# Where the second tile's norm stands at a change of sublayer

## The chip, the cores and the metric

The program runs on one core of a Trainium2 chip. TensorE (PE) multiplies and transposes, VectorE (DVE) and ScalarE (ACT) work elementwise, GpSimd (POOL) computes small powers here, SyncE (SP) starts most of the transfers. Each engine takes its instructions in the order in which they stand in its queue, and waits for others by semaphores. The metric is the time of one execution on the device in microseconds (us), as the median of several runs.

## What is computed

Two residual networks one after the other over 256 tokens of 1024 features, in float32: a modulated block of depth 2, and a block of four layers with another mixer each. Cut to the skeleton:

```python
def first_block(x, c, ...):
    for l in range(2):
        mod = (silu(c) @ w_ada[l] + b_ada[l]).reshape(B, 9, D)
        h = modulate(rms_norm(x, norm_gain[l, 0]), mod[:, 0], mod[:, 1])
        x = x + 0.5 * mod[:, 2] * swiglu(h, ...)           # ffn00, ffn10
        h = modulate(rms_norm(x, norm_gain[l, 1]), mod[:, 3], mod[:, 4])
        x = x + mod[:, 5] * hybrid_mixer(h, ...)           # mixer 0, mixer 1
        h = modulate(rms_norm(x, norm_gain[l, 2]), mod[:, 6], mod[:, 7])
        x = x + 0.5 * mod[:, 8] * swiglu(h, ...)           # ffn01, ffn11

def second_block(h, positions, ...):
    for i in range(4):    # short convolution, recurrence, latent attention, short convolution
        h = h + mixer_i(rms_norm(h, mix_norm[i]))
        h = h + swiglu_ffn(rms_norm(h, ffn_norm[i]), ...)
```

`modulate(h, shift, scale)` is `h * (1 + scale) + shift`. The hybrid mixer holds two attentions of eight heads, a pooling branch, and a gated sum of the three. There are fourteen sublayers, and so thirteen changes from one to the next. At the first five (into mixer 0, ffn01, ffn10, mixer 1, ffn11) the norm has a modulation; at the other eight it has a gain alone.

## The kernel before

The 256 tokens are two tiles of 128, tile 0 and tile 1. `tokens(t)` is a generator over the steps of a tile through all fourteen sublayers; `drive` picks which tile takes its next step. A step yields the weight it held TensorE for: 8 for an up product or a projection, 4 for a down product, or it yields a wait. `drive` keeps how far tile 0 is ahead (`done[0] - done[1]`): from `lag` on tile 1 is picked first. A wait `("wait", a, b)` lets tile 0 go on while it is at most `a` ahead, and tile 1 once tile 0 is at least `b` ahead. What `drive` and the generators emit is the program's order; the framework then places the instructions into each engine's queue, by when it thinks that they can run, and in that it may let instructions of different steps pass each other.

A weight granule (`granule`, L223 to L237) is loaded by SP's queue (512 KB) and split into two float32r parts whose sum it is: ScalarE rounds (`hl`, L234), VectorE takes the rest (L235). `product` (L246 to L254) makes three float32r matmuls of each float32 product; one up product of 512 columns is 24 matmuls into a bank `mm`. Down products add into two banks `dn`. Tile 0 splits a weight chunk, and tile 1 uses it after it.

A change of sublayer: after the last down product `residual` (L309) multiplies the result by the gate (L316, where there is one) and adds it to x (`kept`, L317). `row_stats` (L320) squares x on ScalarE (L326), takes the power -0.5 on GpSimd (L330), and, where the norm has a modulation, leaves the normalised rows (VectorE, L334, `xn`). Then `norm_mod` (L337) or `norm_gain` (L353) begins with the wait `CHAIN`: eight transposes on TensorE (`transposes`, L268, into two `tr` banks), eight scalings on ScalarE (L348) and a split (L279 on ScalarE, L281 on VectorE), or for the gain eight multiplications on each (L291, L294). It ends with the wait `READY`. The next product takes those parts.

`CHAIN = ("wait", 7, 10)`: tile 1's norm may be emitted when tile 0 is 10 ahead, that is after tile 0's norm and the first and second product (8 + 8) of the next sublayer. `lag` is set by `lead`, to 8 (`MID`) or 14 (`END`).

Beside this the first block needs the modulation: `ada_cols` (L368) and `ada_row` (L389) load 512 KB each into one of three `araw` buffers and reduce them on VectorE (L376 for shift and scale, L400 for the gate). `fill` hands such tasks out during tile 0's steps, in a list for the sublayers ahead.

In the attention, `attend` (L509) takes a head norm (`head_norm`: reduction L497, power L304 on GpSimd, multiplication L501), transposes the probabilities into `tr` banks, copies them out (L551 on VectorE) and transposes again through matmuls (L560).

Of the kernel before, what the change touches and what calls it, by code (L numbers as in the profile page):

```python
# [15 lines left out]
PSUM = bass.MemoryType.PSUM  # L16
# [12 lines left out]
# ---------------------------------------------------------------- host layout  # L29


def pack(w, kt, cols):
    """Columns `cols` of w [K, N] as granules [K / (128 kt), 128, kt, len(cols)]."""
    w = w[:, cols]
    k, n = w.shape
    return np.ascontiguousarray(w.reshape(k // (P * kt), kt, P, n).transpose(0, 2, 1, 3))


def consts():
    """Matrices that depend on shapes alone, side by side: [128, n]."""  # L40
# [11 lines left out]
def bands():  # L52
    """What a window of tokens adds to each mean less the token itself: [128, 12, 128]."""
# [14 lines left out]
def arrange(a):  # L68
    """The inputs as the program reads them: the same numbers, laid out."""
# [94 lines left out]
# -------------------------------------------------------------------- program  # L164


class Program:
    """Two tiles of 128 tokens, each a generator over its steps. The second follows the first, so that what one
    tile waits for is hidden by products of the other. A step yields the products it held the tensor engine for
    (in tiles of split weights), or a wait: how far tile 0 may be ahead to go on, how far it must be for tile 1."""  # L170
# [20 lines left out]
    # --- tiles  # L191
# [29 lines left out]
    # --- weights: a granule [128, kt, n] from DRAM, as pairs of float32r parts that add up to it  # L221
# [17 lines left out]
    def weight(self, t, key, srcs):  # L239
        """The rows of k-tiles of a weight chunk: split by the first token tile, used by both."""  # L240
# [5 lines left out]
    def product(self, out, xs, ws, start=True, stop=True):  # L246
        """out += sum over k of xs[k].T @ ws[k] in float32: out is [(ap, column slice)]."""
# [16 lines left out]
    def transposes(self, src, n, tag="tr"):  # L264
        """src [128, n * 128] -> PSUM [128, n, 128], block by block."""
# [9 lines left out]
    def split(self, src, n, scale=1.0, tag="s4"):  # L275
        """float32 [128, n, 128] times scale, as float32r parts (lists over n)."""
# [9 lines left out]
    def split_cols(self, src, n, gain):  # L286
        """float32 [128, n, 128] times a gain per partition and block."""
# [11 lines left out]
    def rsqrt(self, ss, scale, n=1):  # L299
        """(ss * scale + EPS) ** -0.5"""  # L300
# [6 lines left out]
    # --- between sublayers: residual, 1 / rms of the rows of x, norm  # L307

    def residual(self, t, acc, mod, normed):  # L309
        """x += acc (times the gate); then 1 / rms, and x / rms where the norm wants that."""  # L310
# [7 lines left out]
        self.row_stats(t, acc, normed)  # L318

# [17 lines left out]
    def norm_mod(self, t, A, B):  # L337
        """Parts of (x / rms * A + B).T by k-tile."""
# [14 lines left out]
    def norm_gain(self, t, gain):  # L353
        """(x * gain).T and 1 / rms, which the products' results are scaled by."""
# [8 lines left out]
    CHAIN = ("wait", 7, 10)  # L363
    READY = ("wait", 0, 16)

    # --- modulation: c_act @ w_ada + b_ada; shift and scale by feature, the gate as a row on every partition

    def ada_cols(self, state, l, s, i, k):  # L368
        """Two blocks of 128 features of the shift or scale."""
# [19 lines left out]
    def ada_row(self, state, l, s, k):  # L389
        """Two k-tiles of the gate, partial sums by partition."""  # L390
# [20 lines left out]
    def ada_tasks(self, l, s, rows):  # L411
        """Steps that leave rows of shift, scale, gate of sublayer s of layer l in self.mods: (heavy, step)."""
# [19 lines left out]
    # --- feed-forward  # L432
# [52 lines left out]
    # --- attention  # L485

    def head_norm(self, ps, heads, factor=None):
        """PSUM [128, heads * dh], times a factor per token (given with its square), over the rms of each head."""
# [15 lines left out]
    def head_cols(self, y, gain, o):  # L504
        """[128 tokens, 512] -> [128 features, 4, 128 tokens] times a gain per feature."""
        self.nc.scalar.activation(o, self.transposes(y, 4), AF.Copy, scale=gain)
        return o

    def attend(self, t, logits, vs, bias_group, done, dv=64, scale=1.0):  # L509
        """Eight heads, four at a time, in steps. bias_group(g): per head what TensorTensor adds to the logits (or,  # L510
# [729 lines left out]
```

## Time and profile before

| | |
|---|---|
| median of 3 runs | 2535.97 us (2534.54 to 2538.55) |
| profiled execution | span 2533.8 us; it is not one of the three, and has no time beside its span |
| TensorE busy | 2430.1 us, 96% |
| VectorE, ScalarE, GpSimd busy | 64%, 50%, 3% |
| TensorE's granted clock | 0.9 or more of full speed in all but two of 40 slices |
| mean traffic | 197 GB/s, 499 MB |

In the profile a row of a timeline is one instruction or a run of the same: its start in us from the beginning of the span, its length, the engine, the line of the kernel, the operation, which tile it writes and which it reads, the shape, the count; in brackets the time for which the engine stood idle ahead of it, and what ended that. L254 are the matmuls of `product`, L268 the transposes. The clock is given as a share of full speed.

### The profile page before, as it was taken

The page shows a single profiled execution, that of the slowest core. Times are in us where ns is not written, and L with a number is a line of the kernel's source. Part 1 is how long each engine was busy: PE and PEld are TensorE (multiplying, and loading weights), DVE is VectorE, ACT ScalarE, POOL GpSimd, SP SyncE. Part 2 cuts the span into 40 slices and gives each one's busy share as a digit, 9 for nine tenths or more (in the row PEclk, how much of TensorE's full clock was granted, in tenths as well). Part 3 has the DMA queues.
Part 4 walks back from the last instruction along what each step waited for, and adds up shares of the span by engine and source line. Part 5 has one row for each costly group of instructions (what it writes and reads, how often), then busy time and mean ns, then how long its engine had stood idle before and what let it go on. Part 6 is the DMA issues. An engine that isn't in the chain of part 4 may idle for free.

```text
span 2533.8 us, 31294 instructions
## 1 busy us (share of the span) xinstructions
PE 2430.1 (96%) x11394; PEld 1989.6 (79%) x11394; DVE 1625.8 (64%) x2504; ACT 1272.7 (50%) x2007; POOL 86.3 (3%) x114
## 2 busy tenths in 40 slices
PE   6999999999999999999999999988998899999999
PEld 4877878878877878887888888776887688888887
DVE  7868687667568557666457654697545755467553
ACT  4535544554454465446445544675545554465443
POOL 0000100000000021000000000000000100000000
PEclk8999999999999999999999999998999999999999
DMA  8888675569568555445555465543553446555551
GB/s 316 327 295 301 228 260 167 177 229 329 181 214 322 187 183 175 134 161 181 190 176 200 155 202 189 172 160 108 200 179 117 133 135 198 166 193 190 202 184 63
DMA packets 137789, 499.02 MB, mean 197 GB/s; under 512 B 15842, under 2 KB 15842, under 8 KB 137635
## 3 DMA queue, kind: packets, MB, share of 16 engines
q1 hardware_dynamic: 135650, 490.86, 56.6%
q0 software_dynamic: 1984, 6.16, 0.8%
q8 instruction: 89, 1.46, 0.2%
q14 instruction: 66, 0.53, 0.1%
HBM read 495.92 MB, written 1.05 MB: 196 GB/s over the span
## 4 chain that ended last, share of the span: by engine, by line
PE 81%; DVE 6%; DMA 2%; ACT 2%; issue 2%; POOL 1%; SPq 0%; DVEq 0%; POOLq 0%; ACTq 0%
PE mm L254 53%; PE dn L254 21%; PE tr L268 3%; DVE hl L235 2%; PE tr L560 1%; POOL tiny L304 1%; DMA araw<-in_w_shift 1%; DMA araw<-in_w_mod 1%; PE tr L912 0%; ACT hl L234 0%; PE tr L254 0%; PE dn L589 0%; DVE s L922 0%; PE tr L408 0%; PE tr L678 0%
## 5 line engine op out<-in xcount | busy, mean ns | idle before, releaser
L254 PE MATMUL mm<-hl,s 128*128 128x512 f32 (+1 forms) x6774 | 1620.3, 395 | 45.2 <-ACT s L279 19.4
L254 PEld LDWEIGHTS mm<-hl,s 128*128 128x128 f32 x6774 | 1268.9, 190 | 319.3 <-ACT s L279 23.8
L235 DVE TENSOR_TENSOR hl<-raw,hl 128x1024 fp32r<-128x1024 f32 (+1 forms) x792 | 950.3, 1216 | 134.5 <-ACT hl L234 33.5
L234 ACT ACTIVATE hl<-raw 128x1024 fp32r<-128x1024 f32 (+1 forms) x792 | 830.2, 1056 | 365.9 <-PE mm L254 166.0
L254 PE MATMUL dn<-hl,s 128*128 128x512 f32 x2712 | 667.6, 397 | 8.9 <-ACT s L279 8.1
L254 PEld LDWEIGHTS dn<-hl,s 128*128 128x128 f32 x2712 | 497.1, 188 | 113.3 <-ACT s L279 10.2
L449 DVE SCALAR_TENSOR_TENSOR s<-mm,tiny,s 128x256 f32<-128x256 f32 x88 | 42.3, 480 | 266.5 <-ACT s L445 266.5
L445 ACT ACTIVATE s<-mm,tiny 128x256 f32<-128x256 f32 x88 | 41.8, 475 | 259.8 <-PE mm L254 259.7
L268 PE MATMUL tr<-kept,s 128*128 128x128 f32 x860 | 145.9, 279 | 14.7 <-DVE s L334 6.4
L268 PEld LDWEIGHTS tr<-kept,s 128*128 128x128 f32 x860 | 112.9, 144 | 54.7 <-DVE s L334 6.2
L445 ACT ACTIVATE s<-mm 128x256 f32<-128x256 f32 x88 | 33.6, 382 | 213.9 <-PE mm L254 213.9
L376 DVE CUSTOM_DVE_ANT_0 araw<-araw,s 128x1024 f32<-128x1024 f32 x88 | 107.0, 1218 | 38.9 <-DMA araw<-in_w_shift 23.4
L447 DVE TENSOR_TENSOR s<-mm,s 128x256 f32<-128x256 f32 x88 | 36.9, 420 | 133.8 <-ACT s L445 133.8
L281 DVE TENSOR_TENSOR s<-tr,s 128x256 fp32r<-128x256 f32 (+1 forms) x188 | 81.1, 432 | 43.4 <-ACT s L279 43.2
L279 ACT ACTIVATE s<-tr 128x256 fp32r<-128x256 f32 (+1 forms) x196 | 78.5, 401 | 40.7 <-PE tr L268 40.7
L330 POOL TENSOR_TENSOR tiny<-tiny,kept 128x1 f32<-128x1 f32 x30 | 19.7, 658 | 1960.4 <-DVE tiny L328 1930.8
L400 DVE SCALAR_TENSOR_TENSOR acc<-araw,kept,acc 128x1024 f32<-128x1024 f32 x48 | 61.5, 1280 | 11.7 <-DMA araw<-in_w_mod 11.2
L538 ACT ACTIVATE s<-s,tiny 128x128 f32<-128x128 f32 (+1 forms) x80 | 35.4, 444 | 51.2 <-DVE tiny L535 48.2
L326 ACT ACTIVATE dn<-kept 128x512 f32<-128x512 f32 x60 | 35.9, 598 | 49.6 <-DVE kept L317 49.6
L294 DVE SCALAR_TENSOR_TENSOR s<-tr,kept,s 128x128 fp32r<-128x128 f32 x154 | 42.9, 343 | 16.6 <-ACT s L291 16.6
L777 ACT ACTIVATE s<-mm 128x512 f32<-128x512 f32 x24 | 14.3, 597 | 73.7 <-PE mm L254 73.7
L317 DVE TENSOR_TENSOR kept<-kept,dn 128x512 f32<-128x512 f32 x56 | 36.9, 681 | 22.1 <-PE dn L254 21.9
(177 smaller groups left out, 999.6 us busy)
## 6 DMA issues: line engine op xcount, KB each, us to landing
raw<-in_gu SPq DMA_DIRECT2D x352, 512.0 KB, 5.4
raw<-in_dn SPq DMA_DIRECT2D x176, 512.0 KB, 5.9
raw<-in_win SPq DMA_DIRECT2D x104, 512.0 KB, 5.3
araw<-in_w_scale SPq DMA_DIRECT2D x48, 512.0 KB, 7.5
araw<-in_w_mod SPq DMA_DIRECT2D x48, 512.0 KB, 6.9
raw<-in_cin SPq DMA_DIRECT2D x48, 512.0 KB, 5.2
araw<-in_w_shift SPq DMA_DIRECT2D x40, 512.0 KB, 7.6
raw<-in_wbr SPq DMA_DIRECT2D x24, 512.0 KB, 5.5
```

Source lines behind the costliest of these rows:

```text
L234: nc.scalar.activation(hi, raw, AF.Copy)
L235: nc.vector.tensor_sub(lo, raw, hi.bitcast(F32))
L254: nc.tensor.matmul(ap, lhsT=x, rhs=w[:, sl], start=start and k == 0 and i == 0, stop=stop and k == last and i == 2)
L268: self.nc.tensor.transpose(bank[:, j, :], src[:, j * P : (j + 1) * P], self.ident)
L279: nc.scalar.activation(hi, src, AF.Copy, scale=scale)
L281: nc.vector.tensor_sub(lo, src, hi.bitcast(F32))
L294: nc.vector.scalar_tensor_tensor(lo[:, j, :], src[:, j, :], g, hi[:, j, :].bitcast(F32), op0=ALU.mult, op1=ALU.subtract)
L317: nc.vector.tensor_add(x[:, sl], x[:, sl], acc[j])
L376: nc.vector.tensor_tensor_reduce(out=raw, in0=raw, in1=self.crow, scale=1.0, scalar=0.0, op0=ALU.mult, op1=ALU.add, accum_out=state["sum"] ...
L400: nc.vector.scalar_tensor_tensor(acc, raw, self.cact[:, q : q + 1], acc, op0=ALU.mult, op1=ALU.add)
L445: nc.scalar.activation(h, ps[:, :256], AF.Silu, scale=1.0 if r is None else r)
L449: nc.vector.scalar_tensor_tensor(h, ps[:, 256:], r, h, op0=ALU.mult, op1=ALU.mult)
```

## The change

`CHAIN` is now `("wait", 7, 4)`. `residual` notes that tile 1 has come to the end of a sublayer (`self.ended`), and `drive` then advances tile 1's generator at once, so that it stands at its `CHAIN` wait. While it stands there and the wait allows it, tile 1 is picked first, whatever `lag` says. So tile 1's norm is emitted as soon as tile 0 has made one product (8) of the next sublayer, where two were emitted ahead of it before. The emitted steps at a change were: tile 0 product 1, product 2, tile 1 norm, tile 1 product 1; they are: tile 0 product 1, tile 1 norm, tile 0 product 2, tile 1 product 1. In latent attention the norm moves ahead of the second of two down projections. Nothing else in the sequence of steps differs. Comments are gone too, so that lines after L234 have other numbers (by 1 to 2).

```diff
@@ residual @@
         self.row_stats(t, acc, normed)
+        self.ended = t == 1
@@
-    CHAIN = ("wait", 7, 10)
+    CHAIN = ("wait", 7, 4)
     READY = ("wait", 0, 16)
@@ drive @@
         self.lag = self.MID
+        self.ended = False
...
         while any(alive):
-            first = 1 if done[0] - done[1] >= self.lag else 0
+            chain = wait[1] is self.CHAIN and may(1)
+            first = 1 if chain or done[0] - done[1] >= self.lag else 0
             t = next(t for t in (first, 1 - first, "stuck") if t == "stuck" or may(t))
...
             else:
                 done[t] += got
+                if t == 1 and self.ended:
+                    self.ended = False
+                    wait[t] = next(gens[t], None)
+                    alive[t] = wait[t] is not None
```

TensorE's queue at the change from mixer 0 to ffn01, before. `mm_4172` is tile 0's second product, `tr_4212` and `tr_4217` are the transposes of tile 1's normalised rows, `mm_4238` is tile 1's first product, `tr_4200` and `tr_4318` belong to tile 0's activations.

```order
L254 MATMUL mm_4172<-hl_4168,s_896_4053 128x512 x2
L254 MATMUL mm_4172<-hl_4169,s_896_4053 128x512
L254 MATMUL mm_4172<-hl_4168,s_896_4053 128x512
L268 MATMUL tr_4200<-kept,s_914_4130 128x128 x2
L268 MATMUL tr_4212<-kept,s_900_4079 128x128 x4
L268 MATMUL tr_4217<-kept,s_900_4079 128x128 x4
L268 MATMUL tr_4318<-kept,s_933_4197 128x128 x2
L254 MATMUL mm_4238<-hl_4083,s_941_4227 128x512
```

The same place after the change, where `mm_4105` is tile 0's first product and `mm_4198` its second; `tr_4148` and `tr_4153` are tile 1's rows:

```order
L255 MATMUL mm_4105<-hl_4101,s_896_4053 128x512 x2
L255 MATMUL mm_4105<-hl_4102,s_896_4053 128x512
L255 MATMUL mm_4105<-hl_4101,s_896_4053 128x512
L269 MATMUL tr_4148<-kept,s_900_4079 128x128 x4
L269 MATMUL tr_4153<-kept,s_900_4079 128x128 x4
L255 MATMUL mm_4198<-hl_4176,s_894_4045 128x512
L255 MATMUL mm_4198<-hl_4177,s_894_4045 128x512
```

Tile 1's transposes have moved from behind the second product to behind the first, and the 24 matmuls of the second product now stand between them and tile 1's first product.

VectorE's queue in the attention of mixer 1, before. `tiny_8105` is the head norm's mean square, the copy (L551) empties the bank `tr_8131`, and L501 is the multiplication that needs GpSimd's power.

```order
L235 TENSOR_TENSOR hl_8394<-raw_8391,hl_8393 128x1024
L542 RECIPROCAL tiny_8074<-tiny_8069 128x4
L564 TENSOR_TENSOR s_1698_7765<-tr_8124,tiny_7785 128x256
L497 TENSOR_REDUCE tiny_8103<-s_1784_8101 128x8
L302 TENSOR_SCALAR tiny_8105<-tiny_8103 128x8
L551 COPY s_1791_8130<-tr_8131 128x512
L501 TENSOR_TENSOR s_1784_8101<-mm_8076,tiny_8107 128x512
L294 SCALAR_TENSOR_TENSOR s_1789_8115<-tr_8110,kept,s_1789_8115 128x128 x4
```

The same place after the change, where L553 is the copy, L503 the multiplication and L402 a gate's step of the modulation:

```order
L236 TENSOR_TENSOR hl_8394<-raw_8391,hl_8393 128x1024
L402 SCALAR_TENSOR_TENSOR acc_9590<-araw_9692,kept,acc_9590 128x1024
L544 RECIPROCAL tiny_8074<-tiny_8069 128x4
L499 TENSOR_REDUCE tiny_8103<-s_1784_8101 128x8
L566 TENSOR_TENSOR s_1698_7765<-tr_8124,tiny_7785 128x256
L303 TENSOR_SCALAR tiny_8105<-tiny_8103 128x8
L295 SCALAR_TENSOR_TENSOR s_1789_8115<-tr_8110,kept,s_1789_8115 128x128
L503 TENSOR_TENSOR s_1784_8101<-mm_8076,tiny_8107 128x512
L295 SCALAR_TENSOR_TENSOR s_1789_8115<-tr_8110,kept,s_1789_8115 128x128 x3
L553 COPY s_1791_8130<-tr_8131 128x512
```

The copy has moved from ahead of the multiplication to behind it and three more multiplications, and a gate's step stands ahead of all. In the whole program VectorE's modulation instructions have moved: between tile 1's residuals there were 28 in mixer 0 and 8 in mixer 1, and there are 24 in each; the reductions of shift and scale that stood ahead of a change now stand behind it.

## Rows read from the trace of the kernel before

**Rows 1.** The page: busy time, share of the span, instructions.

```profile
PE 2430.1 (96%) x11394; PEld 1989.6 (79%) x11394; DVE 1625.8 (64%) x2504; ACT 1272.7 (50%) x2007; POOL 86.3 (3%) x114
```

**Rows 2.** TensorE's timeline into ffn01: start, length, what; idle ahead in brackets.

```profile
503.39 8.78 PE L254 MATMUL mm<-hl,s 128*128 128x512 f32 x38
...
514.28 1.53 PE L268 MATMUL tr<-kept,s 128*128 128x128 f32 x12
517.56 1.21 PE L254 MATMUL mm<-hl,s 128*128 128x512 f32 x4 [1.75 <-ACT s L279]
```

**Rows 3.** TensorE's timeline at tile 1's norm, other changes of sublayer.

```profile
251.27 0.63 PE L268 MATMUL tr<-kept,s 128*128 128x128 f32 x4 [1.44 <-DVE s L501]
...
253.65 2.61 PE L254 MATMUL mm<-hl,s 128*128 128x512 f32 x6 [1.01 <-DVE s L281]
...
907.72 1.21 PE L254 MATMUL mm<-hl,s 128*128 128x512 f32 x4 [1.64 <-ACT s L279]
909.84 1.65 PE L254 MATMUL mm<-hl,s 128*128 128x512 f32 x3 [0.91 <-DVE s L281]
...
1355.67 1.66 PE L254 MATMUL mm<-hl,s 128*128 128x512 f32 x6 [1.22 <-ACT s L291]
...
1763.30 0.73 PE L254 MATMUL mm<-hl,s 128*128 128x512 f32 x2 [0.46 <-ACT s L291]
...
1951.72 0.73 PE L254 MATMUL mm<-hl,s 128*128 128x512 f32 x2 [2.81 <-ACT s L291]
```

**Rows 4.** Stretches: from:to, length, TensorE busy (instructions), granted clock, DMA share, GB/s.

```profile
234.00:236.50 2.50, 2.50 (x10) 0.50 0.94 329
254.00:257.00 3.00, 3.00 (x9) 0.51 0.60 184
910.00:912.50 2.50, 2.50 (x6) 0.50 0.94 274
343.50:347.50 4.00, 4.00 (x20) 0.50 0.48 138
```

**Rows 5.** Timelines of VectorE and GpSimd, tile 1's residual and normalised rows, into ffn01.

```profile
504.32 0.69 DVE L317 TENSOR_TENSOR kept<-kept,dn 128x512 f32<-128x512 f32 x1
...
508.04 0.75 DVE L334 TENSOR_SCALAR s<-kept,tiny 128x1024 f32<-128x1024 f32 x1 [0.74 <-POOL tiny L330]
...
507.45 0.56 POOL L330 TENSOR_TENSOR tiny<-tiny,kept 128x1 f32<-128x1 f32 x1 [11.55 <-DVE tiny L328]
```

**Rows 6.** ScalarE's timeline, scalings of tile 1's norm into ffn01.

```profile
515.13 1.86 ACT L348 ACTIVATE s<-tr,mod,mod 128x128 f32<-128x128 f32 x5
```

**Rows 7.** Timelines of TensorE (tile 0's norm), VectorE and GpSimd, into mixers 0 and 1.

```profile
231.91 1.20 PE L254 MATMUL dn<-hl,s 128*128 128x512 f32 x4 [2.33 <-ACT s L279]
...
889.13 0.63 PE L268 MATMUL tr<-kept,s 128*128 128x128 f32 x4 [1.45 <-DVE s L334]
...
243.32 1.22 DVE L376 CUSTOM_DVE_ANT_0 araw<-araw,s 128x1024 f32<-128x1024 f32 x1
...
243.41 1.53 POOL L330 TENSOR_TENSOR tiny<-tiny,kept 128x1 f32<-128x1 f32 x1 [11.34 <-DVE mod L386]
```

**Rows 8.** Stretches from tile 1's residual to the next: mixer 0, then mixer 1.

```profile
239.80:503.70 263.90, 256.07 (x1341) 214.01 (x1340) 187.07 (x342) 132.06 (x226) 21.76 (x19) 0.97 0.62 211
...
896.00:1151.10 255.10, 252.17 (x1339) 210.84 (x1338) 162.01 (x280) 131.33 (x225) 19.50 (x19) 0.99 0.49 163
```

**Rows 9.** Timelines of TensorE and VectorE in the attention, mixer 0, then mixer 1.

```profile
343.37 3.68 PE L560 MATMUL tr<-s,s 128*128 128x64 f32 x16 [4.77 <-DVE s L551]
...
342.64 0.68 DVE L551 COPY s<-tr 128x512 f32<-128x512 f32 x1
...
993.74 2.00 PE L560 MATMUL tr<-s,s 128*128 128x64 f32 x16 [0.38 <-DVE s L551]
...
993.00 0.68 DVE L551 COPY s<-tr 128x512 f32<-128x512 f32 x1
994.93 0.69 DVE L501 TENSOR_TENSOR s<-mm,tiny 128x512 f32<-128x512 f32 x1 [1.25 <-POOL tiny L304]
```

## The prediction

> **What bounds the kernel now.** I read the share of busy time first, then TensorE's own timeline around each change of sublayer, then the clock there, then the sublayers side by side. TensorE is busy 96% of the span [rows 1], so only the idle rest, and the stretches in which it runs at half speed, can be won. The 512-column products run at 0.23 us each (38 in 8.78 us), so one product of the next sublayer, 24 of them, holds TensorE for 5.5 us [rows 2]. The timeline of the change from the first mixer to ffn01 shows what the change is about: TensorE goes from tile 0's last down product through the first and second product of the next sublayer, transposes tile 1's input at 514.28, and then stands 1.75 us until ScalarE has turned the transposes into tile 1's operands [rows 2]. ScalarE needs 1.86 us for five of the eight scalings alone [rows 6]. Nothing of tile 0 is left to run there, since its second product came before the norm.
>
> **The change part by part.** No arithmetic is added or taken away, and the norm issues no DMA, so nothing is queued differently on SP or on GpSimd by the norm itself. Three things move.
>
> (1) *Tile 1's norm, thirteen times.* Its transposes now stand behind the first product, and the second product (5.5 us) runs while ScalarE and VectorE work on them. That covers the 1.75 us. The waits that go, change by change [rows 2, 3]: into mixer 0, 1.44 + 1.01; into ffn01, ffn10 and ffn11, 1.75 each (three alike, one row stands); into mixer 1, 1.64 + 0.91; into the short convolution after ffn11, 1.22; five later changes at least 0.46 each (one row stands); one change shows no wait. Without latent attention this is 2.45 + 5.25 + 2.55 + 1.22 + 2.3 = 13.8 us. Into latent attention the wait is 2.81, but what follows there is a chain of small steps, so that between nothing and all of it goes; I take half, 1.4. Sum of the waits: 15.2 us, between 13.8 and 16.6.
>
> (2) *The clock behind these waits.* After the waits into both mixers TensorE's granted clock stands at half, the lower of its levels (1.2 of 2.4 GHz), for 3.0 us from 254 and 2.5 us from 910 [rows 4]. At half speed half of that is lost: 1.5 + 1.25 = 2.75 us, which comes back if TensorE doesn't stand there. The other changes show no such stretch.
>
> (3) *Modulation work.* VectorE's reductions for the next sublayer's shift and scale (1.22 us each [rows 7]) move too, which the diff doesn't say: the order after the change has them behind the boundary, one sublayer later. Counted between tile 1's residuals, mixer 0 goes from 28 modulation instructions of full width (reductions and gate steps) to 24, and mixer 1 from 8 to 24. Two consequences.
>
> At the change into mixer 0 none of them stands any more in tile 0's own norm, where TensorE waits 2.33 us now and where the clock is at half for 2.5 us from 234. The same place at the change into mixer 1 has 1.45 us [rows 4, 7]. Gain: 2.33 - 1.45 + 1.25 = 2.1 us, between 0 and 3.6. At the same change GpSimd's power for tile 1 took 1.53 us, against 0.56 elsewhere [rows 5, 7]: a reduction had begun 0.09 us ahead of it. That is gone too, and is part of what makes (1) possible there. The Trainium skill says so in general (SBUF — State Buffer, "Who interferes with whom"): a VectorE instruction with two SBUF inputs and a GpSimd one that reads SBUF take turns, and the later one waits for the whole of the other. By that page the reductions that now stand in mixer 1 would each be able to hold one of its GpSimd powers by up to 1.2 us, which would put the sum at 2525 instead of 2524; the two rows agree with it.
>
> In the mixers it costs. Mixer 0 holds TensorE for 263.9 us and mixer 1 for 255.1 [rows 8], with the same products; the largest piece of the difference is one wait of 4.77 us against 0.38 at the same place of the attention [rows 9]. The transposes that wait there need a PSUM bank that a VectorE copy empties. In mixer 1 that copy begins at 993.00, ahead of a multiplication that then waits 1.25 us for GpSimd's power; in mixer 0 it stands behind that multiplication and begins at 342.64. The order after the change has the copy behind the multiplication in both mixers, and a gate's step (1.2 us) ahead of them. So mixer 1 should lose what mixer 0 loses now: 4.77 - 0.38 = 4.4 us of waiting and 2.0 us for the 4 us at half clock behind it [rows 4]. For the extra step ahead I take half of it in each mixer, 1.2 in all. Sum: 7.6 us. From below the cost is nothing, if the copy isn't what ends the wait after all; from above it is the whole difference and both steps, 8.8 + 2.4 = 11.2.
>
> (4) *A new wait.* The norm's transposes now stand 5.5 us sooner in TensorE's queue, and all of tile 0's second product stands behind them. Into ffn01 tile 0's first product ends at 503.39 + 24 x 0.23 = 508.9; tile 1's normalised rows are ready at 508.04 + 0.75 = 508.8 [rows 2, 5]. It is a tie, at five changes (those whose norm has a modulation). The other eight need only x itself, which at the place shown is ready at 504.32 + 0.69 = 505.0, well ahead [rows 5]. I take 0.1 us for each of the five, 0.5 us in all. The bounds: nothing, or about 1 us each if GpSimd's power takes 1.53 again, so 5 us.
>
> (5) What gets nothing: splitting the weights of the second and third product. It keeps its order, and ScalarE and VectorE have the 5.5 us of the second product for the norm's eight scalings (3.0 us by [rows 6]) and its splits. If that cover were too short, the second half of tile 1's operands would be late by the remainder, up to 1.75 us a change, which is the kernel as before.
>
> Sum: 15.2 + 2.75 + 2.1 - 7.6 - 0.5 = 12.0 us less. The profiled span is 2533.8 us; the median of the three timed runs is 2536.0, 2.2 us more for what lies around the span. 2536.0 - 12.0 = 2524.0.
>
> **The rivals.**
> - *The gain without the cost.* The copy in mixer 1 turns out to be early enough in the new order: 2536.0 - 20.0 + 0.5 = 2516. For it: one wait of this size in 2,500 us may be a coincidence of that place. Against: VectorE is 187 us busy in mixer 0 and 162 us in mixer 1 [rows 8], and mixer 1 gets that work now. Chance 0.14.
> - *The gain is given back.* Both mixers lose the upper bound (11.2) and the tie of (4) is lost at all five changes (5 us): 2536.0 - 20.0 + 11.2 + 5 = 2532. Here TensorE is kept as busy at the changes as I say, and the time comes back as waits for VectorE in the attention. Chance 0.16, with 0.02 more for the case in which the second product covers nothing, so that the time stays at 2536.
> - *Slower: tile 1's rows come late.* The place is the transposes of (4) at the five changes with modulation. TensorE takes its work in order, so each microsecond by which the rows are late is a microsecond in which tile 0's second product waits too, where before two products stood ahead. A wait of 2.33 us was followed by 2.5 us at half clock [rows 4, 7], that is 1.25 us more. With my other terms the sum turns slower by 0.2% (5 us) once the five changes cost (12.0 + 5.0)/5 = 3.4 us each, so from about 2.1 us late with the clock; 2.5 us late gives 2536.0 - 12.5 + 5 x 3.75 = 2542. For it: the tie, with no reserve. Against: nothing in the order after stands newly between x and these rows. Chance 0.10.
>
> **How the numbers follow.** The forecast, 2524, has 0.58; its own range is 2519 to 2530, from the bounds of the clock and mixer terms. About 0.2% (5 us) is what a measurement of this kernel can tell from no change, so faster means under 2531. Faster: 0.58 + 0.14 = 0.72; same: 0.18; slower: 0.10. The range that should hold the time 8 times in 10 goes from the first rival to the end of the second, 2516 to 2535; outside it lie the slower case and the edges of the others.
>
> **What would show it.** In the profile of the changed kernel: (1) The waits of [rows 2, 3] are gone or under 0.3 us, the one into latent attention at least halved, and the transposes at each change are followed by tile 0's second product without a gap. (2) The half-speed stretches at 254 and 910 are gone. (3) Mixer 1 (between the residuals of tile 1) takes 259 us or more instead of 255, with a wait of 3 to 6 us for a copy in the attention. (4) No wait over 0.3 us at the transposes of tile 1's norm into ffn01, ffn10 and ffn11. I am wrong if the mixers keep their spans (then 2516), if TensorE waits for the normalised rows (VectorE's multiplication at the end of the row statistics) at the changes, or if a wait appears that none of these steps names, most of all in the recurrence and in latent attention, whose order on VectorE and ScalarE also moves a little.

## The result, and the profile after

The median went from 2536.14 us (four runs, 2534.54 to 2538.55) to 2510.47 us (four runs, 2510.04 to 2510.99). The ratio is 0.9899, with an interval of 0.9885 to 0.9913: 25.7 us less, where 12.0 were forecast. The time lies below the range (2516 to 2535), and below the rival of the gain without cost. The profiled execution took 2510.79 us, with a span of 2508.9.

Busy time of the kernel after, from the page (it answers to [rows 1]): TensorE does the same 11394 instructions in 13.5 us less.

```profile
PE 2416.6 (96%) x11394; PEld 1983.5 (79%) x11394; DVE 1627.2 (65%) x2504; ACT 1271.2 (51%) x2007; POOL 88.8 (4%) x114
```

TensorE's timeline after, at the change into ffn01 (answers to [rows 2]; columns as there):

```profile
489.84 5.62 PE L255 MATMUL mm<-hl,s 128*128 128x512 f32 x24
495.30 1.09 PE L269 MATMUL tr<-kept,s 128*128 128x128 f32 x8
496.14 5.72 PE L255 MATMUL mm<-hl,s 128*128 128x512 f32 x24
501.70 0.38 PE L269 MATMUL tr<-kept,s 128*128 128x128 f32 x2
501.84 1.40 PE L255 MATMUL mm<-hl,s 128*128 128x512 f32 x5
```

One product, tile 1's eight transposes, the other product, and no bracket anywhere: neither the old wait of 1.75 us nor a new one for the rows. Into mixer 0 and into latent attention (answers to [rows 3]):

```profile
239.59 10.01 PE L255 MATMUL mm<-hl,s 128*128 128x512 f32 x43
249.44 0.60 PE L269 MATMUL tr<-kept,s 128*128 128x128 f32 x4
...
1926.17 0.55 PE L269 MATMUL tr<-kept,s 128*128 128x128 f32 x3 [0.43 <-ACT s L1015]
1927.07 2.10 PE L255 MATMUL mm<-hl,s 128*128 128x512 f32 x7 [0.36 <-ACT s L292]
```

The 1.44 and 1.01 into mixer 0 are gone; of the 2.81 into latent attention 0.79 is left. The 1.44 was no wait for tile 1's norm, though: in [rows 3] it ends with the head norm's multiplication (L501). It went all the same. GpSimd's power for tile 1 at the change into mixer 0, which took 1.53 us in [rows 7], after:

```profile
237.11 0.55 POOL L332 TENSOR_TENSOR tiny<-tiny,kept 128x1 f32<-128x1 f32 x1 [10.41 <-DVE tiny L705]
```

Stretches of the kernel after, columns as in [rows 4] and [rows 8]: the two places whose clock was at half (tile 0's norm and tile 1's norm into mixer 0), then mixer 0 and mixer 1 between the residuals of tile 1.

```profile
234.00:236.50 2.50, 2.50 (x12) 2.07 (x12) 2.50 (x4) 2.13 (x5) 0.00 (x0) 1.00 0.50 188
249.00:255.00 6.00, 6.00 (x30) 4.96 (x29) 4.64 (x6) 2.24 (x4) 2.95 (x5) 1.00 1.02 409
...
234.50:490.10 255.60, 250.58 (x1339) 210.35 (x1337) 179.79 (x324) 131.56 (x224) 21.99 (x19) 0.99 0.59 200
...
879.80:1132.30 252.50, 249.44 (x1339) 209.50 (x1338) 179.75 (x324) 131.52 (x225) 21.67 (x19) 0.99 0.58 199
```

VectorE's busy time in the two mixers is now alike (180 us each; 187 and 162 before), as the moved modulation work would have it. Yet mixer 0 is 8.3 us shorter and mixer 1 is 2.6 us shorter; mixer 1 was to be longer. The attention of mixer 0, after (TensorE, then VectorE; answers to [rows 9]), and two new waits, one behind the pooling branch of each mixer (L560, here L562, is no transposition: it multiplies the turned probabilities with the values, into a `tr` bank):

```profile
307.92 1.22 PE L255 MATMUL mm<-hl,s 128*128 128x512 f32 x2 [4.81 <-ACT s L654]
...
332.86 1.33 PE L562 MATMUL tr<-s,s 128*128 128x64 f32 x11
...
333.57 0.68 DVE L553 COPY s<-tr 128x512 f32<-128x512 f32 x1
...
950.97 0.74 PE L255 MATMUL mm<-hl,s 128*128 128x512 f32 x2 [3.06 <-ACT s L654]
```

The product L562 runs at 332.86, before the copy L553 that it waited 4.77 us for in the kernel before has even begun (333.57). So the copy is late, as I said, and no longer matters. In its place a projection waits 4.81 us for L654, ScalarE's copy of the pooling branch's first result out of PSUM.

By sublayer (from one residual of tile 1 to the next; the change of the span against the terms of the prediction, us):

| | forecast | measured | measured less forecast |
|---|---|---|---|
| ffn00 (holds tile 0's norm into mixer 0) | -2.1 | -5.3 | -3.2 |
| mixer 0 (waits 2.45, clock 1.5, step +0.6) | -3.35 | -8.3 | -4.95 |
| ffn01, ffn10, ffn11 | -5.25 | -5.1 | +0.15 |
| mixer 1 (waits 2.55, clock 1.25, copy +7.0) | +3.2 | -2.6 | -5.8 |
| the eight with a gain alone | -4.9 | -3.7 | +1.2 |
| new wait at five changes | +0.5 | 0 | -0.5 |
| sum | -11.9 | -25.0 | -13.1 |

The miss is in the two mixers (10.8 us), and 3.2 in ffn00.

### The profile page after: what moved, and what is told of

It is laid out like the page before. It is cut to its first block, busy times and chain, and to the rows that moved or that the text cites. A ratio compares the mean times of both kernels' runs of the same rounds, so it can differ in the third digit from the quotient of the medians.

```text
span 2508.9 us, 31294 instructions
## 1 busy us (share of the span) xinstructions
PE 2416.6 (96%) x11394; PEld 1983.5 (79%) x11394; DVE 1627.2 (65%) x2504; ACT 1271.2 (51%) x2007; POOL 88.8 (4%) x114
## 4 chain that ended last, share of the span: by engine, by line
PE 80%; DVE 4%; issue 2%; ACT 2%; DMA 1%; POOL 1%; SPq 0%; DVEq 0%; POOLq 0%; ACTq 0%
PE mm L255 53%; PE dn L255 21%; PE tr L269 3%; DVE hl L236 1%; PE tr L562 1%; ACT hl L235 1%; POOL tiny L305 0%; PE tr L914 0%; DVE s L924 0%; PE dn L591 0%; DMA araw<-in_w_scale 0%; DVE araw L378 0%; PE tr L680 0%; PE dn L1069 0%; PE tr L410 0%
## 5 line engine op out<-in xcount | busy, mean ns | idle before, releaser
L255 PE MATMUL mm<-hl,s 128*128 128x512 f32 (+1 forms) x6774 | 1618.5, 394 | 37.9 <-ACT s L280 11.6
L255 PEld LDWEIGHTS mm<-hl,s 128*128 128x128 f32 x6774 | 1266.6, 189 | 308.7 <-ACT s L280 15.0
L255 PE MATMUL dn<-hl,s 128*128 128x512 f32 x2712 | 666.8, 397 | 9.6 <-ACT s L280 9.2
L255 PEld LDWEIGHTS dn<-hl,s 128*128 128x128 f32 x2712 | 497.3, 188 | 112.3 <-ACT s L280 11.5
L449 DVE TENSOR_TENSOR s<-mm,s 128x256 f32<-128x256 f32 x88 | 36.9, 420 | 127.3 <-ACT s L447 127.3
L402 DVE SCALAR_TENSOR_TENSOR acc<-araw,kept,acc 128x1024 f32<-128x1024 f32 x48 | 61.4, 1280 | 20.5 <-DMA araw<-in_w_mod 20.2
L540 ACT ACTIVATE s<-s,tiny 128x128 f32<-128x128 f32 (+1 forms) x80 | 35.4, 444 | 47.5 <-DVE tiny L537 47.5
L305 POOL TENSOR_TENSOR tiny<-tiny,kept 128x8 f32<-128x8 f32 (+2 forms) x28 | 46.0, 1644 | 191.7 <-DVE tiny L303 149.0
```

The source lines that it names most:

```text
L255: nc.tensor.matmul(ap, lhsT=x, rhs=w[:, sl], start=start and k == 0 and i == 0, stop=stop and k == last and i == 2)
L305: self.nc.gpsimd.tensor_tensor(r, v, self.minus_half[:, :n], op=ALU.pow)
L402: nc.vector.scalar_tensor_tensor(acc, raw, self.cact[:, q : q + 1], acc, op0=ALU.mult, op1=ALU.add)
```

## The experiments

**How the modulation work came to move.** The diff says nothing of it, and "emitted earlier" doesn't explain it. The addresses in the built programs do: the framework rotates a tag over as many slots as it finds tiles alive at once. Tag `mod` (the sums of shift and scale) has four slots before and two after, since tile 1's norm, which reads them, is emitted earlier (of the two runs below that move one kind of norm, e3, which leaves the norms with a modulation late, has four, and e7, which moves them, has two). With two, a new sum takes over the slot that tile 1's norm still reads, and its reductions stand behind that norm. That can be set by hand, and so the two halves of the change can be run apart.

*Place alone*: the change, with four slots as before. *Reductions alone*: the kernel before, with two.

```diff
# e1_place_alone (in the kernel after)     # e2_reductions_alone (in the kernel before)
-    BUFS = {"raw": 5, "hl": 21, "araw": 3}
+    BUFS = {"raw": 5, "hl": 21, "araw": 3, "mod": 4}     # e2: "mod": 2
```

> The changed kernel with four slots for the sums of shift and scale in place of the two that the allocator gives it. The reductions stand ahead of the change of sublayer again, as in the kernel before (35, 21, 16, 16 and 0 in the first five sublayers, where the changed kernel has 24 and four times 16); the norm keeps its new place. Theory A (the gain is the norm's place, some 20 us with the clock, and the reductions' new place, some 5 us, mostly ffn00 and mixer 0): 2515 us, with the 4.9 us wait for the copy in mixer 0's attention back, and mixer 1 at 249 to 250 us. Theory B (all of the gain is the norm's place, and the reductions' move cost something in mixer 1): 2506 to 2510 us.

> The kernel before with two slots for the sums of shift and scale: the reductions stand behind the change of sublayer, as in the changed kernel, and the norm stays behind the second product. Theory A: 2531 us, ffn00 3 to 5 us shorter, mixer 0 about 4 us shorter, mixer 1 1 to 3 us longer, and all thirteen waits at the changes of sublayer still there. Theory B: 2536 to 2541 us. By my prediction's own term (the reductions cost 7.6 us in the mixers and give 2.1 us at tile 0's norm): 2541 us.

Measured: place alone 2515.18 us, 0.9912 (0.9897 to 0.9927), 21.6 less than before; reductions alone 2534.61 us, 0.9990 (0.9979 to 1.0001), 2.2 less, no clear difference. Counted in the built programs, the reductions stand in e1 as before and in e2 as after. So most of the gain is the place (21.6 of 25.7 us), as theory A said of e1; e2 lies between its expectations. Where the prediction had -17.5 for the place (terms 1, 2 and 4) it gives -21.6, and where it had +5.5 for the reductions (term 3) they give -2.2.

TensorE in the attention, place alone: the old wait for the copy stands as before.

```profile
342.36 0.48 PE L562 MATMUL tr<-s,s 128*128 128x64 f32 x1 [4.73 <-DVE s L553]
```

TensorE at the same product, reductions alone, mixer 0 and mixer 1:

```profile
337.31 0.85 PE L560 MATMUL tr<-s,s 128*128 128x64 f32 x6 [3.13 <-DVE s L501]
...
990.22 0.53 PE L560 MATMUL tr<-s,s 128*128 128x64 f32 x2 [3.08 <-DVE s L501]
```

In the second, mixer 1 takes 261.4 us instead of 255.1: 6.3 longer, almost what I had charged it (6.4 without the extra step). The kernel isn't longer, since ffn00 gets 4.2 and mixer 0 3.2 us shorter in the same profile. But mixer 1 waits for the multiplication L501, not for the copy L551. The same product, in the same place of the code, is held by another instruction. The question is what it waits for.

**The banks.** PSUM, into which TensorE's products go, has eight banks here, two for `mm`, four for `dn`, two for `tr`; but the built program shares each of the eight between all three tags, by which tile is free at that point of the program. A product waits for the last reader of whatever had its bank before. Read from the addresses of the built programs, with the wait from the trace, for four products of mixer 0 (projection, L254 or L255; the pooling branch's second product, L656 or L658; the scores, L591; the product of the turned probabilities, L560 or L562); the scores of e8 are those of mixer 1:

```
kernel   product          bank was before          last read by                       wait, us
before   probabilities    the turned block's tr    VectorE copy L551                  4.77
e1       probabilities    the turned block's tr    VectorE copy L553                  4.73
e2       probabilities    a projection's mm        VectorE multiplication L501        3.13
after    probabilities    the scores' dn           VectorE maxima, long before        none
after    projection       the pooling's first tr   ScalarE copy L654                  4.81
before   projection       an older tr              read long before                   none
e8       projection       a dn                     read long before                   none
e8       pooling's 2nd    the turned block's tr    VectorE copy L553                  3.40
e9       pooling's 2nd    the turned block's tr    VectorE copy L551                  3.61
e10      probabilities    the turned block's tr    ScalarE copy L553                  0.58
e8       scores           a projection's mm        VectorE multiplication L503        1.96
e10      scores           a projection's mm        VectorE multiplication L503        1.37
```

So the wait that I carried from mixer 0 to mixer 1 is not tied to that product: it needs the bank that a late instruction empties, and the change dealt the banks anew.

**Is it the copy?** In the kernel with the place alone, and in the kernel after, the copies out of the `tr` banks go to ScalarE (e5 has e1's four slots also):

```diff
-                nc.vector.tensor_copy(pT[:, i * 4 : i * 4 + 4, :], ps)
+                nc.scalar.activation(pT[:, i * 4 : i * 4 + 4, :], ps, AF.Copy)
```

> As e1 (the norm's new place, four slots, so that the reductions stand where they did before), with the copies of the transposed probabilities in the attention on ScalarE in place of VectorE, so that they stand behind no multiplication that waits for GpSimd. Theory (the 4.9 us wait in mixer 0's attention, with 3 us at half clock behind it, comes from VectorE's queue ahead of that copy): the wait goes, mixer 0 takes 253 us instead of 261, and the kernel 2507 us against 2515 of e1. Rival (the wait is for something else that ends at the same time, such as the probabilities themselves): mixer 0 stays at 259 to 261 us, the kernel at 2513 to 2516.

> The changed kernel (two slots, reductions behind the change of sublayer), with the same copies on ScalarE. There TensorE waits 5.0 and 3.2 us for a ScalarE copy some 25 us ahead of that place in each mixer, and not for the VectorE copies. Theory (that earlier wait has already spent the time, so that the VectorE copies are no longer what is late): nothing is gained, 2509 to 2512 us, with the earlier waits still there. Rival (the copies are late there too, and hide behind the earlier waits, so that these go as well): 2503 us.

Measured: e5 2513.46 us, 0.9902 (0.9887 to 0.9918); e6 2512.32 us, 0.9899 (0.9886 to 0.9913). In e5 the wait of 4.73 is gone and mixer 0 falls from 260.8 to 255.4, but mixer 1 rises by 2.1: its 0.38 at the copy went, and the scores wait 1.74 us for the multiplication L503 there (0.58 in e1), with 1.7 us lost at half clock behind it. Against e1 the kernel gains 1.7 us by the medians; the intervals of the two ratios overlap, so that no gain is shown where 8 us were expected. TensorE, e5, mixer 1:

```profile
962.27 0.93 PE L591 MATMUL dn<-s,s 64*128 64x128 f32 x10 [1.74 <-DVE s L503]
```

In e6 nothing is gained, as expected, though the reason I gave for it (an earlier wait has used up the time) is replaced by the banks: the product doesn't wait for the copy there. The other wait stays: 3.06 us in mixer 1, as in the kernel after, and 2.41 instead of 4.81 in mixer 0. TensorE, e6:

```profile
307.70 0.50 PE L255 MATMUL mm<-hl,s 128*128 128x512 f32 x1 [2.41 <-ACT s L654]
...
956.02 0.72 PE L255 MATMUL mm<-hl,s 128*128 128x512 f32 x2 [3.06 <-ACT s L654]
```

**Is it ScalarE's copy L654?** It is short, but it stands in ScalarE's queue behind four exponentials (L540), which wait for VectorE's maxima and their sign (L537). VectorE and ScalarE, kernel after:

```profile
293.18 1.22 DVE L378 CUSTOM_DVE_ANT_0 araw<-araw,s 128x1024 f32<-128x1024 f32 x1
...
297.75 1.22 DVE L378 CUSTOM_DVE_ANT_0 araw<-araw,s 128x1024 f32<-128x1024 f32 x1
...
300.92 0.69 DVE L503 TENSOR_TENSOR s<-mm,tiny 128x512 f32<-128x512 f32 x1 [1.40 <-POOL tiny L305]
...
303.69 0.16 DVE L537 TENSOR_SCALAR tiny<-tiny 128x4 f32<-128x4 f32 x1
...
303.89 0.51 ACT L540 ACTIVATE s<-s,tiny 128x256 f32<-128x256 f32 x1 [4.85 <-DVE tiny L537]
...
307.29 0.58 ACT L654 ACTIVATE s<-tr 128x512 f32<-128x512 f32 x1
```

Four modulation reductions (the first and the last are shown) and a wait of 1.40 us for GpSimd's power stand ahead of L537. TensorE had finished the tile that L654 reads at 301.6, and the copy begins at 307.29. So the moved reductions have a part in a wait after all, by way of ScalarE, at a place that the prediction doesn't name; how large a part was not run by itself. To take the wait away, the pooling branch's copy goes to VectorE, in the kernel after and in the one before:

```diff
-        nc.scalar.activation(d, ps, AF.Copy)
+        nc.vector.tensor_copy(d, ps)
```

> The changed kernel with the pooling branch's copy out of its transposes' bank on VectorE in place of ScalarE. With this the allocator gives the product that waits 5.0 and 3.2 us in the two mixers another PSUM bank (5, last read by VectorE's maxima) than that of the pooling branch's transposes (1), and the product of the probabilities a bank that no copy empties late. Theory (which earlier tile had the same bank decides what these products wait for; the reductions only make those readers late): both waits go, and the half speed behind them; mixer 0 takes 248 to 250 us instead of 255.6, mixer 1 248 to 249 instead of 252.5, the kernel 2501 to 2504 us. Rival (the attention's chain on VectorE is late by the reductions, whatever the bank): a wait of 3 to 5 us for VectorE stands at the same product, and the kernel stays at 2509 to 2513 us.

> The kernel before with the same copy on VectorE; norm and reductions stand where they stood. The product of the probabilities in mixer 0 then has bank 0 in place of bank 5, which the copy empties; in mixer 1 it has bank 7, and so has the tile that the copy empties there. Theory of the banks: the wait of 4.9 us in mixer 0 goes, with 3.1 us of half speed; the one in mixer 1 (0.5 us) stays under 1 us or grows a little; mixer 0 takes 256 us instead of 264, the kernel 2528 to 2530 us. Rival: mixer 0 keeps a wait of 3 to 5 us there, and the kernel stays at 2535 to 2538 us.

Measured: e8 2510.98 us, 0.9910 (0.9895 to 0.9925), the same as after; e9 2526.79 us, 0.9966 (0.9952 to 0.9980). TensorE, e8, mixers 0 and 1:

```profile
319.19 0.58 PE L658 MATMUL tr<-s,s 128*128 128x128 f32 x1 [3.40 <-DVE s L553]
...
966.32 0.38 PE L658 MATMUL tr<-s,s 128*128 128x128 f32 x1 [1.88 <-DVE s L553]
...
955.60 1.20 PE L591 MATMUL dn<-s,s 64*128 64x128 f32 x16 [1.96 <-DVE s L503]
```

TensorE, e9, mixer 0:

```profile
328.86 0.58 PE L656 MATMUL tr<-s,s 128*128 128x128 f32 x1 [3.61 <-DVE s L551]
```

In e8 the waits of 4.81 and 3.06 are gone, as expected, and the time isn't. Moving one copy dealt the banks anew again: a third product came to stand on the bank that the copy L553 empties, and a fourth, the scores, on one that the multiplication L503 reads last. The expectation had gone by the first two products' banks alone. Of 7.9 us, 3.40 + 1.88 + 1.96 = 7.2 came back, so that the rival's time came true: mixer 0 is 1.4 us shorter than after, and mixer 1, which has 1.7 us more of half clock, 2.6 longer.

In the kernel before (e9), the same edit takes the old 4.77 away and puts 3.61 at that third product. But its expectation is wrong in one point: the reductions don't stand where they stood. The build gives tag `mod` three slots, and in the trace mixer 0 has 16 reductions instead of 21, and mixer 1 has 8 instead of none. So the place of the wait can be read from e9; what its 8.9 us (3.9 of them in mixer 0) are made of can't.

**Both copies exchanged**: e8's edit and e6's edit together, so that the third product's bank is emptied by ScalarE.

> The changed kernel with both: the pooling branch's copy on VectorE, and the copies of the transposed probabilities on ScalarE. The tiles that met late readers so far no longer share a bank with them: the product behind the pooling branch has a bank last read by VectorE's maxima, the pooling branch's second product another than the copies, and the product of the probabilities the bank that a copy empties, but on ScalarE, where no multiplication is in front. Theory of the banks: no wait over 2.5 us at the three places in either mixer, mixer 0 at 249 to 252 us, mixer 1 at 248 to 251, the kernel at 2502 to 2507 us. Rival (the attention's chain is late by the reductions whatever the banks, and only changes the place of its wait): a wait of 3 us or more at another place of each mixer, the kernel at 2509 to 2513 us.

Measured: 2511.90 us, 0.9894 (0.9877 to 0.9911), the same as after. TensorE, e10, mixer 0: the longest of what is left.

```profile
312.17 0.60 PE L591 MATMUL dn<-s,s 64*128 64x128 f32 x6 [1.37 <-DVE s L503]
...
328.56 0.66 PE L562 MATMUL tr<-s,s 128*128 128x64 f32 x4 [0.58 <-ACT s L553]
```

Stretches of e10: mixer 0, the half-clock stretch in mixer 1, and one each in ffn01 and ffn10.

```profile
235.70:485.90 250.20, 248.25 (x1339) 208.46 (x1338) 174.18 (x314) 136.40 (x234) 23.72 (x19) 1.00 0.60 205
...
914.00:922.00 8.00, 8.00 (x27) 6.56 (x27) 6.47 (x11) 6.20 (x8) 1.54 (x1) 0.57 0.97 354
546.00:550.00 4.00, 4.00 (x13) 3.13 (x12) 0.70 (x4) 0.00 (x0) 0.00 (x0) 0.58 1.01 408
733.00:738.00 5.00, 5.00 (x17) 3.90 (x16) 5.00 (x6) 2.12 (x2) 0.00 (x0) 0.66 0.59 208
```

Mixer 0 gains the 5.4 us that were expected of it. The kernel doesn't. The scores in mixer 1 wait 1.57 us in place of the old 3.06, but that mixer has 3.4 us at half clock, 8.0 x (1 - 0.57), where after has 1.7. Both feed-forwards lose 1.7 at half clock, each behind a wait for a VectorE multiplication (L449) that is longer than any there in the kernel after (1.10 and 1.25 us). They lie in sublayers that the edit doesn't touch:

```profile
959.60 0.94 PE L591 MATMUL dn<-s,s 64*128 64x128 f32 x12 [1.57 <-DVE s L503]
...
545.05 3.48 PE L255 MATMUL mm<-hl,s 128*128 128x512 f32 x9 [3.18 <-DVE s L449]
...
732.33 3.09 PE L255 MATMUL mm<-hl,s 128*128 128x512 f32 x9 [2.74 <-DVE s L449]
```

So the theory of the banks holds for the three places that it named, and the rival got the time right, with waits of half the size that it gave. No version that I ran is clearly faster than the kernel after.

**The two kinds of norm apart, and the norm still earlier.** `LATER` is the wait of before, and stands in place of `CHAIN` in one of the two norms of the kernel after; in e4 the norm may go ahead of every product.

```diff
# e3_gain_norms_only: in norm_mod          # e7_mod_norms_only: in norm_gain
-        yield self.CHAIN
+        yield self.LATER
...
+    LATER = ("wait", 7, 10)
# e4_norm_first
-    CHAIN = ("wait", 7, 4)
+    CHAIN = ("wait", 7, 0)
```

> The norm of tile 1 follows the first product only at the eight changes whose norm has a gain alone; at the five with a modulation it stays behind the second product, and the reductions stand as in the kernel before. Both theories: 2532 us (the eight sublayers gave 3.8 us between the two profiles: 1.5, 0.7, -1.1, 0.7, 0.1, 0.7, 0.4, 0.7). My prediction's terms for these eight (1.2 + 5 x 0.46 + 1.4) say 4.9 us: 2531 us. Over 2535 us would mean that the eight places give nothing.

> The counterpart of e3: the norm of tile 1 follows the first product at the five changes with a modulation, and stays behind the second at the eight with a gain alone. The reductions stand behind the change, as in the changed kernel. If the thirteen places add up: the changed kernel and what e3 gave for the eight, 2510.5 + 7 = 2517 us by e3's times, 2515 by the sublayers of its profile (4.6 us).

> The changed kernel with the norm emitted ahead of the first product too. In TensorE's order the transposes still stand behind most of the first product at the changes with a modulation, since the framework places them where it thinks that the rows are ready. If emission only has to be early enough and the framework's placing does the rest: 2508 to 2513 us. If the place of emission itself sets when TensorE has to wait for the normalised rows, which are ready 5.4 us after tile 0's last down product: 5 x 5.4 us more, about 2537 us.

Measured: e3 2529.62 us, 0.9970 (0.9961 to 0.9980), 7.2 less; e7 2520.66 us, 0.9927 (0.9914 to 0.9939), 17.4 less. Together 24.6, against 25.7 for all thirteen: the two kinds add up. By the prediction's terms the eight with a gain were worth 4.9 and the five with modulation 15.2 - 4.9 + 2.75 + 2.1 - 7.6 - 0.5 = 7.0. So about 10 of the 13 us missed are in the five. I expected a few us more of e7.

e4 gave 2530.52 us, 0.9974 (0.9964 to 0.9984): still faster than before, but 20 us slower than after, and between the two expectations. TensorE, e4, mixers 0 and 1:

```profile
256.30 0.50 PE L255 MATMUL mm<-hl,s 128*128 128x512 f32 x1 [2.76 <-DVE hl L236]
...
340.80 0.48 PE L562 MATMUL tr<-s,s 128*128 128x64 f32 x1 [3.98 <-DVE s L553]
...
911.34 0.80 PE L255 MATMUL mm<-hl,s 128*128 128x512 f32 x1 [2.72 <-DVE hl L236]
...
992.66 0.69 PE L562 MATMUL tr<-s,s 128*128 128x64 f32 x2 [2.32 <-DVE s L553]
```

The framework left the transposes behind the first product, so that at the changes TensorE waits 0.8 us at most for the rows. The time is lost in the two mixers (some 11 us each against after): late weight splits at their start, and the banks dealt as in the kernel before, with the copy's wait now long in both. It is the loss I had forecast for mixer 1 (2.32 and half clock behind it), in a kernel that does have that bank.

## Why the prediction was wrong

(1) *Thirteen waits, 15.2 us.* Right in place and about right in size: none is left but 0.79 of the 2.81. In ffn01, ffn10 and ffn11 the sublayers give 5.1 of the 5.25, though spread (+0.4, -3.0, -2.4): in ffn01 the 1.75 went, and TensorE's waits for the multiplication L449 grew from 0.29 to 2.35 us. The eight others give 7.2 where they alone change (e3; 5.8 in those sublayers of its profile), and 3.7 in the profile of after: the recurrence gets 1.1 longer there, and has more half clock than before.

(2) *Clock behind the waits, 2.75 us.* Right, a little too small. I had cut the stretches short: over the whole of it, length times (1 - granted clock), each cost 1.7 us. Both are gone. Stretches of before, at full length: the attention of mixer 0, tile 1's norm into mixer 0 and into mixer 1, and two that I hadn't counted at all.

```profile
342.00:350.00 8.00, 6.63 (x30) 6.24 (x31) 7.22 (x15) 0.00 (x0) 0.00 (x0) 0.57 0.67 230
254.00:258.00 4.00, 4.00 (x12) 3.15 (x11) 2.86 (x6) 0.42 (x1) 3.17 (x4) 0.57 0.69 220
909.00:913.50 4.50, 3.66 (x10) 2.96 (x11) 2.61 (x4) 1.43 (x2) 2.21 (x5) 0.62 0.80 228
281.00:285.00 4.00, 4.00 (x12) 3.09 (x11) 0.28 (x2) 2.98 (x4) 0.00 (x0) 0.57 0.92 294
936.00:941.00 5.00, 5.00 (x16) 3.93 (x16) 0.41 (x3) 2.98 (x4) 0.00 (x0) 0.66 0.86 297
```

The ones at 281 and 936, 1.7 us each, are gone after (e1 still has the first). No wait of TensorE stands just ahead of them. What it ran there is 24 small matmuls of eight columns; but the kernel after runs the same 24 at two places with the clock at full, so that what set them off stays open. TensorE and the clock, before, then after:

```profile
277.57 2.82 PE L254 MATMUL tr<-s,s 128*128 128x8 f32 x24
...
933.05 2.82 PE L254 MATMUL tr<-s,s 128*128 128x8 f32 x24
...
267.08 2.82 PE L255 MATMUL tr<-s,s 128*128 128x8 f32 x24
...
267.00:285.00 18.00, 18.00 (x105) 15.16 (x104) 12.47 (x26) 10.10 (x14) 4.00 (x3) 1.00 0.92 320
```

Summed over the whole span, length times (1 - granted clock) is 37.4 us before and 29.4 after: 8.0 of the 25 us (at most, since in some of it TensorE stood idle), where terms 2 and 3 together had 2.0.

(3a) *Tile 0's norm into mixer 0, 2.1 us.* Right in kind: the half clock at 234 is gone, and so is the long power (0.55 us instead of 1.53). The 2.33 in [rows 7] was a wait for the split of ffn00's last activations (ScalarE L279), not for tile 0's norm; it is gone too. Where 2.33 and 0.38 us of waits stood, 0.77 and 0.67 stand after, so that about 1.3 us of waiting went. ffn00 gave 5.3. Part of that isn't this term's: another 1.7 us stretch at 155 is missing after, though TensorE's wait there is no shorter (2.73 us, 2.40 before). The two halves point to the reductions' place: ffn00 is 4.2 us shorter where they alone move (e2), and 2.2 longer where they stay (e1).

(3b) *The mixers, 7.6 us lost: the step that failed.* The sentence that fell is "so mixer 1 should lose what mixer 0 loses now". Its parts were right: the reductions moved, the copy went behind the multiplication, and in [rows 9] the product did wait for that copy. The prediction even named the tie, a PSUM bank that the copy empties. It took for granted that the product would get the same bank in the new program, and the banks are dealt anew in each build. In the kernel after, neither mixer waits for the copy: where all terms together left the two mixers as long as they were (-3.35 + 3.2), they are 10.9 us shorter. What mixer 0 lost there it doesn't lose any more (4.77, and 3.4 at half clock); 4.81 and 3.06 for L654 stand there instead, with 8.0 x (1 - 0.57) = 3.4 and 5.0 x (1 - 0.66) = 1.7 at half clock:

```profile
306.00:314.00 8.00, 6.08 (x16) 4.84 (x17) 6.84 (x20) 2.91 (x5) 1.64 (x1) 0.57 0.79 285
951.00:956.00 5.00, 5.00 (x15) 3.94 (x16) 3.84 (x14) 0.86 (x1) 1.64 (x1) 0.66 0.91 346
```

The two waits in mixer 0 cancel (4.81 for 4.77), so that the changes' own waits (2.45) and 3.4 us less of half clock are left, and some 2.4 of its 8.3 us that I can't name. In mixer 1, 2.55 of waits went and 3.06 came (0.38 at the copy went too), with 1.7 less of half clock: about 1.6 of its 2.6. That banks decide where TensorE waits is shown by e2, e6, e8, e9 and e10: in each the wait is where its built program has a late reader's bank. How late the reader is depends on what VectorE has ahead of it, and there the moved reductions do cost: no edit of the banks took the waits away whole, each left some, at the same or at another product. Waits and half clock together account for the mixers of e8 and e10 against after to within about 1 us (e8: -1.6 and +2.5 counted, -1.4 and +2.6 measured).

(4) *New wait, 0.5 us.* It was 0: the rows come in time at all five.

(5) *The splits.* Nothing, as said.

*The rivals.* The gain without cost (2516) was nearest, and its condition held in effect: "the copy in mixer 1 turns out to be early enough" should have read "isn't what holds the bank". That it came nearest is in part luck: 4.81 and 3.06 us for L654 came, which it doesn't have, and against them the 4.77 for the copy in mixer 0 went, and more half clock than it counts. Given back and slower did not occur; e4 is what giving back looks like, with the norm too early.

*What stays open.* The place alone (21.6) gave 4.1 more than its terms, 17.5. Some 1.7 of it lie at seven changes where nothing else moved (ffn11 and behind it all but the recurrence and latent attention): they gave 7.0 us in e1, and the waits counted there were 1.75 + 1.22 + 5 x 0.46 = 5.3, so that by this estimate a stop costs some 0.25 us more than its bracket says. Half clock is part of the rest, but which stretches a run has differs from kernel to kernel also where nothing was edited. Whether the two slots add the 4.7 us between e1 (2515.18) and after (2510.47) isn't shown: the intervals of their ratios overlap.

## What to carry to other kernels

A changed order of emission changes which tiles are alive together, and with it the slots and banks that an allocator deals out. Before pricing a wait in the changed kernel by a wait of the old one, find the buffer that ties the two instructions, and see in the new build which tile had it before and who reads that tile last. Waits that the moved work itself covers (one product of 5.5 us over a chain of 1.75) could be counted from the timeline and came out right; waits at a place that another build decides can't be carried from one sublayer to the next.

## What was not expected of the hardware

In this case's traces a stretch at half clock cost about 1.7 or 3.4 us (the rows above; longer ones in the recurrence): 1.7 behind waits of 1.44 and 1.01 us, 3.4 behind 4.77. It also came where no wait stood ahead, and stayed away behind a wait of 2.73 us. With 28 to 40 us a run, it hides the worth of a single wait of 2 us; it is one reason why a sum of waits doesn't give the time.

GpSimd's power of one column took 1.53 us where a reduction had begun ahead of it and 0.55 at the same place without one. That is the rule of the Trainium skill (SBUF — State Buffer, "Who interferes with whom") that the prediction named. In mixer 1 three of the eight powers of eight columns took 2.14, 2.52 and 2.48 us after, where all took 1.64 to 1.66 before; the only wait of TensorE over 0.2 us there, the 3.06, names ScalarE's copy and not these powers.
